# Forgetting heads' values: two of three column chunks, over half of K, as seven block products in place of eight

## The chip, the cores and the metric

The kernel runs on one core of a Trainium2 chip. The metric is the device time of one execution in microseconds, as the median of several runs: 1101.15 us before the change (three runs, 1100.56 to 1102.84). The core has five engines that run their own instruction streams and wait for each other through semaphores: TensorE (PE: matmuls; PEld is its weight load), VectorE (DVE), ScalarE (ACT), GpSimd (POOL) and SyncE (SP). Most transfers are issued by SP, some by POOL; POOL's can add to their destination.

## What is computed

One layer of a hybrid encoder over 256 tokens of width 2048, all in float32: a normed input times one wide matrix, two groups of eight attention heads, an output projection, and a convolutional feed-forward network.

```python
def hybrid_mixer(h, w_in_l, b_forget_l, ...):
    proj = h @ w_in_l          # 256 x 2048 times 2048 x 6152
    qa, ka, va, fa, qb, kb, vb = jnp.split(proj, splits, axis=-1)
    qa = rms_norm(to_heads(qa, N_HEADS_FOX), q_norm_l)
    ka = rms_norm(to_heads(ka, N_HEADS_FOX), k_norm_l)
    log_f = jax.nn.log_sigmoid((fa + b_forget_l).astype(jnp.float32))
    c = jnp.cumsum(log_f, axis=1).transpose(0, 2, 1)
    out_a = forgetting_attention(qa, ka, to_heads(va, N_HEADS_FOX), c)
    ...
```

The change concerns `va`, the values of the eight forgetting heads (1024 columns), which the kernel computes together with the eight columns `fa` of the forget gates: 1032 columns in three chunks of 344.

## The kernel before

**Products in three.** A float32 operand x is kept as a high part hi, rounded to the matmul's format, and a low part lo = x - hi. A product is then three matmuls: token-high by weight-high, token-low by weight-high, token-high by weight-low (`in_three`, L237). Tokens are the stationary operand: `hT[k]`, k = 0 to 15, holds tile k of K (128 rows) with both parts for all 256 tokens; four of them lie in one buffer, hT_76 to hT_79. Weights stream past with up to 512 columns.

**One piece.** `token_major` (L253) goes over K four tiles at a time. For each such piece, `weights` (L230) loads a raw block (`w_raw`, three buffers, issued by SP), and `split` (L213) makes `w_hi` by a cast on ACT (L220) and `w_lo` by a subtraction on DVE (L221), two buffers each. Then come 24 matmuls (L245): 4 tiles x 3 products x 2 halves of the tokens, into the PSUM tile `acc`. A cast can begin only when TensorE has left the high part of two pieces before; a load only when DVE has done the low part of three pieces before.

**The stage.** After an opening that computes the first half's queries, the kernel computes the values (three chunks of four pieces each, L563 on), the first half's keys, the second half's queries and keys (`project`, 512 columns, four pieces each), then the other attention group. Values leave PSUM by `values` (L550): token half 0 as a high and a low part in `vA`, token half 1 in float32 in `vA_rest`. The gates go through `gates` (L576).

**Work beside it.** Small work is written as Python generators that `step()` (L188) moves on by one piece each time; so it is woven between the pieces. `fox_rows` (L332) takes a row set of 512 query or key columns from PSUM (`raw`), squares and sums it over each head on DVE (L343, L345), takes the root (`rsqrt`, L108: two tiny ACT operations, the rest on DVE), rescales (L348), and some steps later transposes it by TensorE (`to_heads`, `ps_h`, L324). `fox_head` (L636) makes scores `ps_s`, weights `pr`, and their transposes `ps_p` (L628), whose high parts ACT and whose low parts DVE (L633) write to `pT`; one step later `weighted` (L606) multiplies them with the values into `ps_o` (L612). Heads go in pairs: 0 and 1, then 2 and 3. `row1` and `R1` (L689, L690) are tiny transfers on POOL that spread `rstd1`, the tokens' norm factors, over all partitions.

**What sets the order.** TensorE runs in the order in which the program is written. On ACT, DVE, SP and POOL a scheduler sets the order when the program is built; `high_priority` moves an instruction ahead in it, `issue_after` holds one behind another. Each engine then runs strictly in that order, and an instruction that waits holds all behind it on its engine.

**Seven in place of eight.** The output projection has such a product already (`in_seven`, L835). A 2 x 2 product of blocks (two halves of the tokens, two halves of K, two halves of the columns) takes eight block products; with sums and differences of token blocks and of weight blocks it takes seven. One block product is 12 matmuls (four tiles of K, three products, one half of the tokens). The token sums are made by DVE and split into `sums` (`block_sums`, `block_parts`); the weight sums are made in place in `w_sum`, in part by POOL's adding transfers.

Of the kernel before, what the change touches and what calls it, by code (L numbers as in the profile page):

```python
# [15 lines left out]
P = 128  # L16
# [30 lines left out]
def hybrid_layer(  # L47
# [59 lines left out]

    def rsqrt(out_, ss, scale, n):  # L108
# [4 lines left out]
        act.activation(y, a, AF.Ln)  # L113
        act.activation(y, y, AF.Exp, scale=-0.5)
        dve.tensor_tensor(u, a, y, op=ALU.mult)
        dve.tensor_tensor(u, u, y, op=ALU.mult)
        dve.tensor_scalar(u, u, -0.5, 1.5, op0=ALU.mult, op1=ALU.add)
        dve.tensor_tensor(out_, y, u, op=ALU.mult)
# [13 lines left out]
    hT = [None] * KT  # L132

    def new_tokens(g):
        t = big.tile([P, 4, 2, S], F32R, name=f"hT{g}", tag=f"hT{g}")
        hT[4 * g : 4 * g + 4] = [t[:, i] for i in range(4)]

# [67 lines left out]
    def load(src):  # L205
        raw = wraw.tile([P, 2048], F32, name="w_raw", tag="w_raw")
        a, b = src.shape[1:]
        nc.sync.dma_start(raw[:, : a * b].rearrange("p (a b) -> p a b", a=a), src)
        return raw

    in_turn, last_split = [], []

    def split(raw, a, b):  # L213
        hi = whi.tile([P, 2048], F32R, name="w_hi", tag="w_hi")
        lo = wlo.tile([P, 2048], F32R, name="w_lo", tag="w_lo")
        n = a * b
        with ExitStack() as turn:
            for ins in in_turn:
                turn.enter_context(tc.issue_after(ins.ins))
            last = [act.copy(hi[:, :n], raw[:, :n])]  # L220
            last.append(dve.tensor_tensor(lo[:, :n], raw[:, :n], f32(hi[:, :n]), op=ALU.subtract))  # L221
        last_split[:] = last
        if in_turn:
            in_turn[:] = last
# [79 lines left out]
    with ExitStack() as actx:  # L304
# [9 lines left out]
        def project(c0, cols):  # L314
            return token_major(lambda k: hT[k], wi, 0, KT, c0, cols)
# [15 lines left out]

        def fox_rows(acc, dst, g, steps=2):  # L332
# [6 lines left out]
            for t in range(NT):  # L339
# [8 lines left out]
                dve.tensor_tensor(r3, r3, r.unsqueeze(2).to_broadcast([P, 4, HD]), op=ALU.mult)  # L348
# [8 lines left out]
        oT_fox = late.tile([P, NH, 2, S], F32R, name="oT_fox")  # L357
        oT = [oT_fox[:, h] for h in range(NH)]
# [4 lines left out]
        def attended(po, h, g, group):  # L363

            if len(done) == NH:
# [175 lines left out]

        qT0 = fox_queries(0)
        waiting.append(fox_rows(acc_q0, qT0, gq, 4))
        step()


        vA_parts = at.tile([P, 2, WF], F32R, name="vA", tag="vA")
        vA = (vA_parts[:, 0], vA_parts[:, 1], vA_rest)
# [8 lines left out]

        lf = at.tile([P, NT, NH], F32, name="lf")
        for j in range(3):
            acc = project(2 * WF + 344 * j, 344)  # L560
            n = 344 if j < 2 else 336
            for t in range(NT):
                if j == 2:  # L563
                    dve.scalar_tensor_tensor(
                        lf[:, t, :], acc[:, t, 336:344], rstd1[:, t : t + 1], bf,
                        op0=ALU.mult, op1=ALU.add,
                    )
            values([v[:, 344 * j : 344 * j + n] for v in vA], acc[:, :, :n])
# [101 lines left out]
        for half in range(2):  # L670
            if half:
                qT = fox_queries(1)
                waiting.append(fox_rows(project(512, 512), qT, gq, 3))
# [4 lines left out]
            waiting.append(fox_rows(project(WF + 512 * half, 512), kT, g_k))  # L678
# [99 lines left out]
        in_order = tc.keep_in_program_order  # L778
        blocks, sums = [], []

        def block_sums():

            for h, tag in enumerate(("minus_c1", "blocks")):
                blocks.append(at.tile([P, 4, S], F32, name=f"oT_blocks{h}", tag=tag))
                some = slice(4 * h, 4 * h + 4)
                in_order(dve.tensor_tensor(
                    blocks[h], f32(oT_fox[:, some, 0, :]), f32(oT_fox[:, some, 1, :]), op=ALU.add
                ))
            a11, a21, a12, a22 = (blocks[h][:, :, t * P : (t + 1) * P] for h in range(2) for t in range(2))
            in_order(dve.tensor_tensor(a11, a11, a21, op=ALU.subtract))  # L790
            in_order(dve.tensor_tensor(a21, a21, a22, op=ALU.subtract))
            in_order(dve.scalar_tensor_tensor(a22, a11, -1.0, a22, op0=ALU.mult, op1=ALU.subtract))
            in_order(dve.tensor_tensor(a12, a12, a22, op=ALU.add))

        def block_parts():
            sums.extend(big.tile([P, NH, S], F32R, name="oT_sums", tag=f"hT{g}") for g in (1, 2))
            places = [[t[:, 4 * h : 4 * h + 4] for t in sums] for h in range(2)]
            for (hi, _), block in zip(places, blocks):
                in_order(act.copy(hi, block))
            for (hi, lo), block in zip(places, blocks):  # L800
                in_order(dve.tensor_tensor(lo, block, f32(hi), op=ALU.subtract))

        for half in range(2):
            qT = sb_queries(half)
            if half:
                block_sums()
# [28 lines left out]
        def in_seven(c0, plus_rg, minus_rg):  # L835

            w11, w12, w21, w22 = (rows_of(wo, 4 * h, 4, c0 + 512 * i, 512) for h in range(2) for i in range(2))
            banks = {}

            def of_heads(h, t):  # L840
                return lambda i, part, _: of_half(oT[4 * h + i], part, t)

            def of_sums(h, t):
                return lambda i, part, _: sums[part][:, 4 * h + i, t * P : (t + 1) * P]

            def plus(into, src):
                with tc.high_priority(offset=AHEAD):
                    nc.gpsimd.dma_start(
                        into.rearrange("p (a b) -> p a b", a=4), src, accum_op=ALU.add
                    )  # L850

            def product(bank, lhs, parts, to, factor=plus_rg):
                new = bank not in banks
                if new:
                    pool, tag = (psb, "t") if bank == "bank_b" else (pss, "s")
                    banks[bank] = pool.tile([P, 512], F32, name=bank, tag=tag)
                in_three([banks[bank]], parts, 4, lhs, new, True, more=not new)
                residual(to[0], c0 + 512 * to[1], banks[bank], factor)

            w, x12 = (  # L860
                pool.tile([P, 2048], F32, name=name, tag=tag)
                for pool, name, tag in ((at, "w_sum", "vA"), (big, "x12", "hT0"))
            )
            with tc.high_priority(offset=AHEAD):
                for into, src in ((w, w11), (x12, w12)):
                    nc.sync.dma_start(into.rearrange("p (a b) -> p a b", a=4), src)
            yield
            yield
            yield
            with tc.issue_after(last_head[0].ins), tc.issue_after(last_head[1].ins):  # L870
                parts = split(w, 4, 512)
                in_order(dve.tensor_tensor(w, w, x12, op=ALU.add))
                block_parts()
            product("bank_a", of_heads(0, 0), parts, (0, 0))
            product("bank_c", of_heads(1, 0), weights(w21, 4, 512), (0, 0))
            yield
            with tc.high_priority(offset=AHEAD):
                parts = split(w, 4, 512)
            plus(w, w22)
            plus(x12, w22)  # L880
            product("bank_b", of_sums(0, 1), parts, (1, 1))
            yield
            product("bank_b", of_sums(1, 0), weights(w22, 4, 512), (0, 1))
            yield
            with tc.high_priority(offset=AHEAD):
                parts = split(w, 4, 512)
            plus(w, w21)
            product("bank_a", of_sums(1, 1), parts, (0, 1), minus_rg)
            yield
            with tc.high_priority(offset=AHEAD):  # L890
                parts = split(x12, 4, 512)
            product("bank_a", of_sums(0, 0), parts, (1, 1), minus_rg)
            yield
            with tc.high_priority(offset=AHEAD):
                parts = split(w, 4, 512)
            product("bank_a", of_heads(1, 1), parts, (1, 0))
# [3 lines left out]
        seven = in_seven(1024, rgs[0], minus_rg)  # L900

        in_turn.extend(last_split)
# [33 lines left out]
    in_turn.clear()  # L936
# [365 lines left out]
```

## Time and profile before

| | |
|---|---|
| median of three runs | 1101.15 us |
| profiled execution, own time | 1100.61 us |
| its span, first to last instruction | 1098.8 us |
| TensorE, DVE, ACT busy | 1094.2, 895.2, 709.3 us |
| granted TensorE clock | 1.0 |
| bytes moved by DMA | 249.04 MB |

The span is 1.8 us shorter than the execution's own time. A row of the timeline gives the start in us from the span's start, the time it took, the engine, the line of the kernel, the operation, what it writes and reads, and the number of equal instructions merged; in brackets stands the idle time of the engine before it and what ended it. A group row gives the busy time, the mean time of one in ns, and the idle time before them. A window row gives the busy time of each engine in that stretch, the granted clock, the mean busy share of the 16 DMA engines, and what they moved. PE rows are modelled to the end of the last matmul, so neighbouring rows overlap by up to 0.2 us.

### The profile page before, as it was taken

What the parts mean: (1) busy time and instruction counts of PE and PEld (TensorE: products, weight loads), DVE (VectorE), ACT (ScalarE), POOL (GpSimd) and SP (SyncE); (2) the same over time, 40 slices, a digit from 0 to 9 for tenths busy, and PEclk for the clock granted to TensorE, in tenths of its full rate; (3) what the DMA queues carried; (4) which work ended last, traced back from release to release, by engine and by line L of the source; (5) the groups of instructions that cost most, each with busy time, mean ns of one, the idle gap of its engine ahead of it and who ended that gap; (6) DMA issues with size and microseconds to landing.
All of it is one profiled execution on the core that took longest, in us unless ns stands there. A gap on an engine that the chain in (4) does not pass through costs nothing.

```text
span 1098.8 us, 14833 instructions
## 1 busy us (share of the span) xinstructions
PE 1094.2 (100%) x5856; PEld 949.3 (86%) x5856; DVE 895.2 (81%) x957; ACT 709.3 (65%) x884; POOL 47.9 (4%) x49
## 2 busy tenths in 40 slices
PE   9999999999999999999999999999999999999998
PEld 7998888888888888888888888888888888888887
DVE  5755777977789776789889988799798889889896
ACT  6544556664665566767757776777676677677753
POOL 0000000000000000001010000100000010100010
PEclk9999999999999999999999999999999999999999
DMA  8776654576639395558999597977979688987985
GB/s 289 183 235 230 190 155 153 192 231 195 226 118 284 110 333 195 168 180 229 278 233 292 191 251 262 259 262 183 320 203 308 211 222 276 248 264 196 324 205 180
DMA packets 180991, 249.04 MB, mean 227 GB/s; under 512 B 4480, under 2 KB 119066, under 8 KB 180666
## 3 DMA queue, kind: packets, MB, share of 16 engines
q1 hardware_dynamic: 162458, 209.67, 58.3%
q0 software_dynamic: 18144, 37.89, 18.4%
q8 instruction: 46, 0.75, 0.3%
q10 hardware_dynamic: 320, 0.53, 0.1%
q14 instruction: 23, 0.19, 0.0%
HBM read 245.97 MB, written 2.11 MB: 226 GB/s over the span
## 4 chain that ended last, share of the span: by engine, by line
PE 100%; ACT 0%; DVE 0%; issue 0%
PE pu L271 34%; PE acc L245 20%; PE pu L277 18%; PE bank_a L245 11%; PE bank_b L245 5%; PE bank_c L245 3%; PE acc L446 2%; PE acc L1180 1%; PE ps_x L146 1%; PE ps_o L612 1%; PE bank_a L1180 1%; PE ps_p L628 0%; PE ps_o L613 0%; PE ps_h L324 0%; PE idle L399 0%; PE ps_s L540 0%
## 5 line engine op out<-in xcount | busy, mean ns | idle before, releaser
L221 DVE TENSOR_TENSOR w_lo<-w_raw,w_hi 128x2048 fp32r<-128x2048 f32 (+1 forms) x194 | 434.9, 2245 | 119.9 <-ACT w_hi L220 119.2
L220 ACT CAST w_hi<-w_raw 128x2048 fp32r<-128x2048 f32 (+1 forms) x194 | 363.6, 1876 | 221.8 <-PE acc L245 61.2
L271 PE MATMUL pu<-hT,w_hi 128*128 128x512 f32 x1664 | 394.0, 390 | 0.0
L271 PEld LDWEIGHTS pu<-hT,w_hi 128*128 128x128 f32 x1664 | 310.3, 188 | 63.1
L277 PEld LDWEIGHTS pu<-hT,w_lo 128*128 128x128 f32 x1664 | 211.9, 191 | 7.0
L277 PE MATMUL pu<-hT,w_lo 128*128 128x256 f32 x1664 | 215.1, 283 | 0.0
L245 PE MATMUL acc<-w_hi,hT 128*128 128x512 f32 (+1 forms) x576 | 124.4, 368 | 0.0
L245 PEld LDWEIGHTS acc<-w_hi,hT 128*128 128x128 f32 x576 | 101.6, 188 | 14.5
L221 DVE TENSOR_TENSOR w_lo<-w_sum,w_hi 128x2048 fp32r<-128x2048 f32 x34 | 77.9, 2290 | 23.1 <-ACT w_hi L220 23.1
L220 ACT CAST w_hi<-w_sum 128x2048 fp32r<-128x2048 f32 x34 | 64.9, 1910 | 46.6 <-PE pu L271 36.4
L997 ACT ACTIVATE tap<-up,ccol 128x256 f32<-128x256 f32 x176 | 74.6, 495 | 0.0
L245 PE MATMUL acc<-w_lo,hT 128*128 128x512 f32 (+1 forms) x288 | 64.6, 366 | 0.0
L245 PEld LDWEIGHTS acc<-w_lo,hT 128*128 128x128 f32 x288 | 51.6, 188 | 7.5
L1102 POOL DMA_DIRECT2D w_sum<-in_w_down_dram x20 | 25.4, 1272 | 678.5 <-DVE w_lo L221 665.4
L245 PE MATMUL bank_a<-w_hi,g 128*128 128x512 f32 x160 | 40.0, 392 | 0.0
L245 PE MATMUL bank_b<-w_hi,s 128*128 128x512 f32 x160 | 40.0, 392 | 0.0
L245 PE MATMUL bank_a<-w_hi,s 128*128 128x512 f32 x160 | 40.0, 392 | 0.0
L245 PEld LDWEIGHTS bank_a<-w_hi,g 128*128 128x128 f32 x160 | 28.9, 189 | 5.3
L245 PEld LDWEIGHTS bank_a<-w_hi,s 128*128 128x128 f32 x160 | 28.9, 189 | 5.3
L245 PEld LDWEIGHTS bank_b<-w_hi,s 128*128 128x128 f32 x160 | 28.9, 189 | 5.3
L1002 DVE TENSOR_TENSOR gate<-gate,tap 128x512 f32<-128x512 f32 x44 | 30.3, 689 | 2.5 <-ACT tap L997 0.2
L1002 DVE TENSOR_TENSOR val<-val,tap 128x512 f32<-128x512 f32 x44 | 30.3, 688 | 2.3
(248 smaller groups left out, 1107.5 us busy)
## 6 DMA issues: line engine op xcount, KB each, us to landing
w_raw<-in_w_up_dram SPq DMA_DIRECT2D x88, 1024.0 KB, 7.6
w_raw<-in_w_down_dram SPq DMA_DIRECT2D x44, 1024.0 KB, 6.0
w_raw<-in_w_in_dram SPq DMA_DIRECT2D x36, 1024.0 KB, 5.5
w_sum<-in_w_down_dram POOLq DMA_DIRECT2D x20, 1024.0 KB, 10.1
w_raw<-in_w_out_dram SPq DMA_DIRECT2D x14, 1024.0 KB, 6.7
w_raw<-in_w_down_dram POOLq DMA_DIRECT2D x10, 1024.0 KB, 14.8
w_raw<-in_w_in_dram SPq DMA_DIRECT2D x12, 688.0 KB, 4.2
w_raw<-in_w_in_dram SPq DMA_DIRECT2D x6, 512.0 KB, 7.0
```

The costliest lines, as they stand in the source:

```text
L146: nc.tensor.transpose(ps[:, j, t * P : (t + 1) * P], xt[t][:, (k + j) * P : (k + j + 1) * P], ident)
L220: last = [act.copy(hi[:, :n], raw[:, :n])]
L221: last.append(dve.tensor_tensor(lo[:, :n], raw[:, :n], f32(hi[:, :n]), op=ALU.subtract))
L245: nc.tensor.matmul(o, lhs(i, l, t), r[:, i, :], start=starts and j == 0, stop=stops and j == 3 * n - 1, skip_group_check=more,)
L271: nc.tensor.matmul(acc[:, j, :], hi[:, i, j * P : (j + 1) * P], hT[k].rearrange("p a b -> p (a b)"), start=k == 0, stop=low_first and k == ...
L277: nc.tensor.matmul(acc[:, j, S:], lo[:, i, j * P : (j + 1) * P], hT[k][:, 0, :], start=False, stop=not low_first and k == KT - 1,)
L446: nc.tensor.matmul(acc[:, t, :], of_half(hT[2 * c + i + j], l, t), r[:, j, :], start=high and c == i == m == 0, stop=not high and c == 7 a ...
L612: nc.tensor.matmul(po, v[j][:, hs], wp[:, k], start=i == 0, stop=False)
L997: act.activation(taps[w][:, j, :], u[:, j, w : w + S], AF.Copy, scale=ccol[:, w, f : f + 1])
L1002: dve.tensor_tensor(a, a, tap, op=ALU.add)
L1102: nc.gpsimd.dma_start(mem[into][:, : nk * 512].rearrange("p (a b) -> p a b", a=nk), src, accum_op=ALU.add)
L1180: nc.tensor.matmul(o, of_half(g, l, t), r[:, i, c0 : c0 + cols], start=kh == 0 and j == 0, stop=kh == n - 1 and j == 11,)
```

## The change

**Values.** Chunks 0 and 1 of the values (columns 0 to 343 and 344 to 687) are computed by `token_major` over tiles 8 to 15 of K only. Over tiles 0 to 7 they are computed by `in_seven`, which is now shared with the output projection and works here on blocks of four tiles of K, 344 columns and 128 tokens. It is a generator (`seven`) that `token_major` moves on by one step after each piece, so its products stand singly between plain pieces of the values, the keys and the second half's queries. Chunk 2, with the gates, stays plain.

```diff
-        for j in range(3):
-            acc = project(2 * WF + 344 * j, 344)
...
+        for c in range(3):
+            k0, nk = (0, KT) if c == 2 else (8, 8)
+            acc = token_major(lambda k: hT[k0 + k], wi, k0, nk, 2 * WF + FIRST * c, FIRST, seven)
             for t in range(NT):
+                if c < 2:
+                    scaled(value_columns[t][c], acc[:, t, :FIRST], t)
+                    continue
```

Called w11, w12, w21, w22 the four weight blocks (first index: half of the eight tiles of K, second: chunk), the sequence is as follows. `in_seven` loads w11 into `w_sum` and w12 into two half buffers `x12` by SP; it multiplies w11 (S1, into bank_a) and w21 (S2, bank_c); DVE adds w12 to `w_sum`; POOL adds w22 to `w_sum` and `x12`, later w21 to `w_sum`; five more products follow, S3 (`w_sum`), S4 (w22), S5 (`w_sum`), S6 (`x12`), S7 (`w_sum`). Each product has its own split, and each is added to the values by a DVE operation.

```diff
+            product("bank_a", of_blocks(0, 0), prepared(lambda: split(w, 4, cols), sum_weights), (0, 0))
+            if not at_once:
+                yield
+                first_loads(moved_x12, (w12,))
+            product("bank_c", of_blocks(1, 0), weights(w21, 4, cols), (0, 0))
...
+            parts = split_ahead(w)
+            moved(nc.gpsimd, w, w22, accum_op=ALU.add)
+            moved_x12(nc.gpsimd, w22, accum_op=ALU.add)
+            product("bank_b", of_sums(0, 1), parts, (1, 1))
+            yield
+            product("bank_b", of_sums(1, 0), weights(w22, 4, cols), (0, 1))
+            yield
+            parts = split_ahead(w)
+            moved(nc.gpsimd, w, w21, accum_op=ALU.add)
+            product("bank_a", of_sums(1, 1), parts, (0, 1), True)
+            yield
+            product("bank_a", of_sums(0, 0), split_ahead(x12), (1, 1), True)
+            yield
+            product("bank_a", of_blocks(1, 1), split_ahead(w), (1, 0))
```

The values are kept in float32 until all products are added; four more casts on ACT and four subtractions on DVE then make the parts in `vA`:

```diff
+            def add(t, h, ps, minus=False):
+                some = value_columns[t][h]
+                factor = (minus_rstd1 if minus else rstd1)[:, t : t + 1]
+                dve.scalar_tensor_tensor(some, ps, factor, some, op0=ALU.mult, op1=ALU.add)
...
+            parts = at.tile([P, 2, WF], F32R, name="vA", tag="vA")
+            for h in range(2):
+                for c0, n, c in ((0, FIRST, FIRST * h), (FIRST, LAST, 2 * FIRST + LAST * h)):
+                    hi, lo = (parts[:, i, c : c + n] for i in range(2))
+                    act.copy(hi, full[h][:, c0 : c0 + n])
+                    dve.tensor_tensor(lo, full[h][:, c0 : c0 + n], f32(hi), op=ALU.subtract)
```

**Squares.** In `fox_rows`, for all four row sets, the squares and their sums move from DVE to ACT:

```diff
-                dve.tensor_tensor(sq, raw, raw, op=ALU.mult)
                 ss = small.tile([P, 4], F32, name="ss", tag="ss")
-                dve.tensor_reduce(ss, sq.rearrange("p (h d) -> p h d", h=4), axis=AX.X, op=ALU.add)
+                for h in range(4):
+                    some = slice(h * HD, (h + 1) * HD)
+                    act.activation(sq[:, some], raw[:, some], AF.Square, accum_out=ss[:, h : h + 1])
```

**Order.** While `ordered[0]` is set, which is now also so from the values to the end of the second half's queries, each split is held behind the last one on ACT and DVE:

```diff
-            for ins in in_turn:
+            for ins in last_split if ordered[0] else ():
                 turn.enter_context(tc.issue_after(ins.ins))
```

The change moves instructions on every engine; the lines shift too (L220 and L221 become L229 and L232, L633 becomes L800, L318 becomes L327). Two places matter below. First, SP's queue at the start of the values. A transfer of 128x4x344 is the raw block of one piece. Before:

```order
L208 DMA w_raw<-in_w_in_dram 128x4x344
L105 DMA masks<-in_cst_dram 128x256
L106 DMA bf<-in_b_forget_dram 128x8
L208 DMA w_raw<-in_w_in_dram 128x4x344 x11
L208 DMA w_raw<-in_w_in_dram 128x4x512 x12
```

And now (`w_sum` receives w11, x_499 and x_500 the halves of w12):

```order
L211 DMA w_raw<-in_w_in_dram 128x4x344
L105 DMA masks<-in_cst_dram 128x256
L106 DMA bf<-in_b_forget_dram 128x8
L211 DMA w_raw<-in_w_in_dram 128x4x344 x2
L612 DMA w_sum<-in_w_in_dram 128x4x344
L211 DMA w_raw<-in_w_in_dram 128x4x344
L612 DMA x_499<-in_w_in_dram 128x2x344
L211 DMA w_raw<-in_w_in_dram 128x4x344
L612 DMA x_500<-in_w_in_dram 128x2x344
L211 DMA w_raw<-in_w_in_dram 128x4x344 x4
L211 DMA w_raw<-in_w_in_dram 128x4x512 x2
L211 DMA w_raw<-in_w_in_dram 128x4x344
```

Three loads without a `w_raw` buffer now stand between those of the pieces, which before were each held until a buffer came free.

Second, ACT and DVE where the second half's keys leave PSUM and heads 2 and 3 get their transposed weights (`pT`). ACT before, and ACT now:

```order
L220 CAST w_hi<-w_raw 128x2048
L318 ACTIVATE raw<-acc,rstd_391 128x512 x2
L631 CAST pT<-ps_p 128x256
L632 COPY pT_1485<-ps_p 128x128
L631 CAST pT<-ps_p 128x256
L632 COPY pT_1494<-ps_p 128x128
L220 CAST w_hi<-w_raw 128x2048
```

```order
L327 ACTIVATE raw<-acc,rstd_390 128x512 x2
L357 ACTIVATE sq,ss<-raw 128x128 x5
L115 ACTIVATE rs_y<-rs_a 128x4
L357 ACTIVATE sq,ss<-raw 128x128
L116 ACTIVATE rs_y<-rs_y 128x4
L357 ACTIVATE sq,ss<-raw 128x128 x2
L798 CAST pT<-ps_p 128x256
L115 ACTIVATE rs_y<-rs_a 128x4
L799 COPY pT_1544<-ps_p 128x128
L116 ACTIVATE rs_y<-rs_y 128x4
L798 CAST pT<-ps_p 128x256
L229 CAST w_hi<-w_raw 128x2048
```

Eight squares and four roots now stand between the row set and the next cast of weights. On DVE the same place before, and now:

```order
L221 TENSOR_TENSOR w_lo<-w_raw,w_hi 128x2048
L343 TENSOR_TENSOR sq<-raw 128x512 x2
L345 TENSOR_REDUCE ss<-sq 128x4 x2
L112 TENSOR_SCALAR rs_a<-ss 128x4
L633 TENSOR_TENSOR pT<-ps_p,pT 128x256
L112 TENSOR_SCALAR rs_a<-ss 128x4
L633 TENSOR_TENSOR pT<-ps_p,pT 128x256
L221 TENSOR_TENSOR w_lo<-w_raw,w_hi 128x2048
```

```order
L361 TENSOR_TENSOR raw<-raw,r 128x512
L117 TENSOR_TENSOR rs_u<-rs_a,rs_y 128x4
L800 TENSOR_TENSOR pT<-ps_p,pT 128x256
L118 TENSOR_TENSOR rs_u<-rs_u,rs_y 128x4
L119 TENSOR_SCALAR rs_u<-rs_u 128x4
L120 TENSOR_TENSOR r<-rs_y,rs_u 128x4
L361 TENSOR_TENSOR raw<-raw,r 128x512
L232 TENSOR_TENSOR w_lo<-w_raw,w_hi 128x2048
L800 TENSOR_TENSOR pT<-ps_p,pT 128x256
```

The low part of head 3's weights (the second `pT`) stood ahead of the low part of the next weight piece, and now stands behind it.

More of the change, by code (lines that the diff above doesn't have):

```diff
@@ L353, in fox_rows @@
             yield
-        oT_fox = late.tile([P, NH, 2, S], F32R, name="oT_fox")
-        oT = [oT_fox[:, h] for h in range(NH)]
+        oT, oT_fox = [], []
         vA_rest = late.tile([P, WF], F32, name="vA_rest", tag="two_heads")
@@ L363, in attended @@
         def attended(po, h, g, group):
+            if not done:
+                oT_fox.append(late.tile([P, NH, 2, S], F32R, name="oT_fox", tag="eight"))
+                oT.extend(oT_fox[0][:, h] for h in range(NH))
             if len(done) == NH:
@@ L672, in hybrid_layer @@
                 qT = fox_queries(1)
[L673 removed]
+                waiting.append(fox_rows(project(512, 512, seven), qT, gq, 3))
+                ordered[0] = False
                 step()
@@ L677, in hybrid_layer @@
             kT = fox_keys(half)
-            waiting.append(fox_rows(project(WF + 512 * half, 512), kT, g_k))
+            waiting.append(fox_rows(project(WF + 512 * half, 512, seven), kT, g_k))
             step()
@@ L776, in sb_head @@
             attended(weighted(v, slice((h % 4) * HD, (h % 4 + 1) * HD), (w, w1)), h, g_sb, 1)
[L778 to L801, printed above, removed]
         for half in range(2):
@@ L805, in hybrid_layer @@
             if half:
-                block_sums()
+                fox_sums = block_sums([oT_fox[0][:, 4 * i : 4 * i + 4] for i in range(2)])
             kT = sb_keys(half)
@@ L833, in residual @@
             dve.scalar_tensor_tensor(xs, ps, factor[:, t : t + 1], xs, op0=ALU.mult, op1=ALU.add)
[L835 to L862, printed above, removed]
-            )
[L864 to L896, printed above, removed]
```

171 lines of the change are left out of this document (147 added, 24 removed).

## The prediction

> **What bounds the kernel now.** I read first the page's busy times and the chain of waits.
>
> ```profile
> PE 1094.2 (100%) x5856; PEld 949.3 (86%) x5856; DVE 895.2 (81%) x957; ACT 709.3 (65%) x884; POOL 47.9 (4%) x49
> PE 100%; ACT 0%; DVE 0%; issue 0%
> ```
>
> TensorE is busy in 1094.2 of 1098.8 us, and the chain that ended last is TensorE throughout. There is no idle time in which a delay could vanish: a matmul taken out is gained, and any wait of TensorE that is put in is paid in full. So I need two things: what the removed products cost, and whether ScalarE (ACT), VectorE (DVE) and the loads still deliver every operand in time. The timeline of TensorE gives the pace (start, us, line, operation, count):
>
> ```profile
> 31.67 2.67 PE L245 MATMUL acc<-w_hi,hT 128*128 128x344 f32 x16
> 34.18 1.43 PE L245 MATMUL acc<-w_lo,hT 128*128 128x344 f32 x8
> 35.44 2.67 PE L245 MATMUL acc<-w_hi,hT 128*128 128x344 f32 x16
> ```
>
> A plain piece of four tiles of K is 24 matmuls of 344 columns, from 31.67 to 35.44: 3.77 us, 0.157 us each.
>
> **Term 1, the products.** Half of K over two chunks is four plain pieces, 96 matmuls; seven block products of 12 are 84. The change removes 12 x 0.157 = 1.9 us, and nothing else leaves TensorE's order. Below I call the plain pieces G0, G1, ... and the block products S1 to S7. With no wait they start at G0 31.67, G1 35.44, G2 39.21, S1 42.98, G3 44.87, S2 48.64, G4 50.53.
>
> **What the other engines get.** The windows of the stage (us, then busy time of PE, PEld, DVE, ACT, POOL, granted clock, DMA share, GB/s):
>
> ```profile
> 31.70:46.80 15.10, 15.10 (x98) 15.08 (x97) 11.39 (x24) 6.66 (x12) 1.84 (x3) 1.00 0.78 141
> 46.80:62.80 16.00, 16.00 (x106) 16.00 (x105) 7.57 (x6) 8.50 (x9) 0.00 (x0) 1.00 0.84 258
> 62.80:78.00 15.20, 15.20 (x98) 15.20 (x98) 7.56 (x5) 6.93 (x7) 0.00 (x0) 1.00 0.74 248
> 78.00:100.40 22.40, 22.40 (x102) 18.13 (x101) 10.78 (x10) 9.91 (x11) 1.59 (x3) 1.00 0.75 247
> L786 DVE TENSOR_TENSOR oT_blocks<-oT_fox 128x1024 f32<-128x1024 f32 x2 | 2.4, 1220 | 0.0
> 51.43 0.57 DVE L554 SCALAR_TENSOR_TENSOR vA<-acc,rstd,vA 128x344 fp32r<-128x344 f32 x1
> 53.29 1.59 DVE L221 TENSOR_TENSOR w_lo<-w_raw,w_hi 128x1376 fp32r<-128x1376 f32 x1 [0.58 <-ACT w_hi L220]
> 48.54 1.35 ACT L220 CAST w_hi<-w_raw 128x1376 fp32r<-128x1376 f32 x1 [5.26 <-DMA w_raw<-in_w_in_dram]
> ```
>
> DVE is busy in 37.3 of 68.7 us, ACT in 32.0. DVE gains three low parts (3 x 1.59), the block sums and their low parts (four operations of 1024 columns at 1.22, four of 512 at about half), two weight sums of 688 (about 0.85 each), seven updates (7 x 0.57) and four small low parts: about 19 us. ACT gains three casts (3 x 1.35), two of 1024, four small ones and the squares of two row sets (below, 6 us): about 14 us. Both still fit, with 12 us and more to spare. So I take all this as hidden, and look for places where the order makes one late operand. I went along each engine's new order, adding these durations, and found three.
>
> **Term 2, the loads of S2 and G4.** Two tiny transfers of `rstd` to DRAM leave POOL at 34.92. Below stand their row of the timeline, three windows around them, then the loads into `w_raw` between 24 and 60 us with their times to landing, and TensorE's row of the piece whose load was latest:
>
> ```profile
> 34.92 1.30 POOL L689 DMA_DIRECT2D row<-rstd  x2 [33.26 <-DVE rstd L118]
> 36.00:37.00 1.00, 1.00 (x8) 1.00 (x7) 1.00 (x1) 0.88 (x2) 0.21 (x1) 1.00 1.05 385
> 38.00:46.00 8.00, 8.00 (x53) 8.00 (x52) 6.98 (x17) 3.24 (x6) 0.54 (x1) 1.00 0.71 29
> 47.00:49.00 2.00, 2.00 (x17) 2.00 (x16) 0.00 (x0) 0.46 (x1) 0.00 (x0) 1.00 1.11 380
> L208 SPq DMA_DIRECT2D w_raw<-in_w_in_dram x9: 367/368/378, 29.1 to 57.1; - x9
> DMA to landing us min/median/max: 4.0/4.4/11.1
> 51.44 2.67 PE L245 MATMUL acc<-w_hi,hT 128*128 128x344 f32 x16
> ```
>
> From 2.6 us after their issue, for some 9 us, the queues move 29 GB/s in place of 380. Before the change one load falls into this: it lands after 11.1 us, its cast waits 5.26 us for it (48.54 above), and its matmuls start at 51.44, 1.5 us after that cast's end. The old kernel stood just clear of this hole. The new one asks for more bytes ahead of it: SP now sends G2 (from 29.1), w11, G3, half of w12, w21 (S2), the other half of w12, G4. A chunk of 688 KB is 0.70 MB, 1.85 us at 380 GB/s. With the first landing at 33.1 (29.1 + 4.0) come w11 at 34.9 and G3 at 36.8. The hole opens about 1 us earlier, near 36.4, because `rstd` now stands ahead of the second low part on DVE; until 45.4 it lets through 0.27 MB. What is left of G3 and w12's half ends near 46.0, w21 at 47.9, w12's rest at 48.8, G4 at 50.6. Each cast adds 1.35: S2's high part is ready at 49.25, 0.6 after 48.64; G4's at 51.95, 0.8 after its start thus shifted. I take 1.4 us. If the hole shuts a microsecond sooner it is 0.4, without the hole 0 (ACT and DVE alone are in time there); a microsecond later, 2.6.
>
> **Term 3, the keys' transposes.** Their rows were finished 0.8 us before use (109.17 + 1.29 against 111.28):
>
> ```profile
> 109.17 1.29 DVE L348 TENSOR_TENSOR raw<-raw,r 128x512 f32<-128x512 f32 x2
> 111.28 1.03 PE L324 MATMUL ps_h<-cs,raw 128*128 128x128 f32 x8
> ```
>
> Two block products now lie between (3.8 us more room), but ACT has squares, a further cast and the value casts there, and DVE's second rescaling stands behind a low part of 2.2 us. Adding up, it ends 0.3 us late; bounds 0 and 0.8.
>
> **Term 4, head 3's weights.** This is the largest, and lies outside the seven products: `fox_rows` now squares on ACT, eight pieces of 128 with their sums in place of two DVE pairs. Where the last of the row sets, the second half's keys, falls beside heads 2 and 3, the engines stood so (rows of the timeline of ACT, DVE, TensorE; then two exponentials on ACT):
>
> ```profile
> 150.24 1.26 ACT L318 ACTIVATE raw<-acc,rstd 128x512 f32<-128x512 f32 x2
> 151.38 0.37 ACT L631 CAST pT<-ps_p 128x256 fp32r<-128x256 f32 x1
> 152.06 0.30 ACT L632 COPY pT<-ps_p 128x128 f32<-128x128 f32 x1
> 154.51 1.91 ACT L220 CAST w_hi<-w_raw 128x2048 fp32r<-128x2048 f32 x1 [2.16 <-PE pu L271]
> 156.33 0.29 ACT L113 ACTIVATE rs_y<-rs_a 128x4 f32<-128x4 f32 x2
> 155.44 0.42 DVE L633 TENSOR_TENSOR pT<-ps_p,pT 128x256 fp32r<-128x256 f32 x1
> 156.49 2.29 DVE L221 TENSOR_TENSOR w_lo<-w_raw,w_hi 128x2048 fp32r<-128x2048 f32 x1 [0.63 <-ACT w_hi L220]
> 158.69 0.23 DVE L115 TENSOR_TENSOR rs_u<-rs_a,rs_y 128x4 f32<-128x4 f32 x2
> 156.73 0.61 PE L612 MATMUL ps_o<-pT,vA 128*128 128x256 f32 x3
> 125.00 0.39 ACT L658 ACTIVATE pr<-pr,nm 128x128 f32<-128x128 f32 x1
> 125.39 0.50 ACT L659 ACTIVATE pr<-pr,nm 128x256 f32<-128x256 f32 x1
> ```
>
> Before, both heads' low parts (`pT`, L633 on DVE) were done at 155.86, the weight's low part followed, and head 3's matmuls began at 156.73. In the new order DVE has the second `pT` behind `w_lo` of 2048, and `w_lo` needs ACT's cast. That cast could not start before 154.51 (TensorE frees its buffer), and now stands behind the squares. In the old clock: rows end at 151.38; eight squares of 128 with a sum, at the 0.39 from one exponential's start to the next (125.00 to 125.39), are 3.1; four tiny roots some 0.45 (0.11 apart); the `pT` copies 0.7: the cast starts at 155.65 and ends at 157.55; `w_lo` takes 2.2 (156.49 to 158.69) to 159.8, `pT` 0.4 to 160.2. Head 3's second matmul, the first to read it, was due at 156.85. TensorE, in order, waits 3.4 us, with all behind it. If the squares were fast enough to clear the cast, order alone leaves 159.1, 2.3 us. If a square takes 0.5, it is 4.2. I take 3.3, nearer the 0.39 row. A shift of everything before this place shifts both sides alike, so earlier stalls give no cover.
>
> **The accumulating transfers** I cost at nothing. POOL adds w22, then w21, into `w_sum`:
>
> ```profile
> L848 POOL DMA_DIRECT2D w_sum<-in_w_out_dram x2: 1268/1270/1271, 335.2 to 351.9; - x2
> DMA to landing us min/median/max: 8.7/10.4/12.1
> ```
>
> There 1024 KB land in 8.7 to 12.1 us; here they are 688 KB. From one use of `w_sum` to the next lie two block products and two plain pieces of 512 columns (5.44 each, 24 x 0.227): 14.7 us of TensorE, plus the 2 us by which the low part leads. Cover 3 us or more. If it were gone, each microsecond late costs one.
>
> **The sum:** -1.9 + 1.4 + 0.3 + 3.3 = +3.1 us; by the bounds from +0.4 (-1.9 + 0 + 0 + 2.3) to +5.7 (-1.9 + 2.6 + 0.8 + 4.2). The profiled execution took 1100.61 us (1.8 outside the span), the median of the runs is 1101.15. So 1103.7 against the first, 1104.2 against the median.
>
> **The rivals.**
>
> - *The hole is covered* (+1.7 us, 1102.9): terms 1, 3 and 4 alone. For it: the exact length of the hole decides, and I have one sample. Against: 2.1 MB are sent before G3 has landed, where 1.4 were. 0.16.
> - *Full saving, not slower* (-1.9 us, 1099.3): DVE reaches the second `pT` before the weights' low part counts, and the loads keep their lead. Its place is 156.73; it decides from the point where `w_lo` starts 3.4 us sooner than I reckon. Against it: the cast was released by TensorE only at 154.51 even before. 0.04; with only one of the two waits gone for good (no wait at the heads, 1100.9) another 0.03.
> - *TensorE loses its pace after the long wait* (1105.9). In the opening, after idling, 14 matmuls of 256 columns took 3.17 us:
>
> ```profile
> 1.06 3.17 PE L399 MATMUL idle<-zeros 128*128 128x256 bf16 x14 [1.06 <-DVE zeros L389]
> 154.32 2.08 PE L277 MATMUL pu<-hT,w_lo 128*128 128x256 f32 x16
> ```
>
>   That is 0.21 each against 0.12 later, for about 4 us: 1.7 us lost. If a wait of 3.4 us sets TensorE back to it, it costs 1.7 more. Against: no wait in this trace is long enough to show it. 0.06. The Trainium skill, "TensorE: Matmul & The Clock Gate", Part 1, has the rule: the clock is halved after an idle window of 3413 ns, free-running; by it a gap of about that length seldom fills a whole window, and the trace here shows only the opening's slow pace.
> - *The accumulations come late* (1108): landing twice as slow, 21 us against 17, twice. 0.05.
>
> **The numbers.** Forecast 0.66, with its own range 1102.4 to 1106.2. Predicted 1104.2. Reaching down to the covered hole and half-way to the lower cases, up past the slow pace: 1101.4 to 1107.0. About 0.2% (2.2 us) is what a measurement can tell; slower begins at 1103.35. Slower: 0.53 of the forecast, 0.04 of the covered hole, the two last rivals 0.11: 0.68. Faster, below 1098.95: half of the full saving, 0.02, and a little of scatter: 0.04. Same: 0.28.
>
> **What would show it.** TensorE idle at head 3's `ps_o` matmul, released by DVE's `pT`, 2.3 to 4.2 us: term 4. Idle before bank_c and the next plain piece, released by ACT's cast that itself waited for a load: term 2; released by DVE instead, my load ledger is wrong. A small gap at `ps_h`: term 3. 5844 matmuls in place of 5856. A gap before bank_a would be the late accumulations. Wrong altogether if TensorE stays without gaps.

## The result, and the profile after

| | before | after |
|---|---|---|
| median | 1101.09 us (9 runs, 1100.56 to 1102.84) | 1104.93 us (9 runs, 1102.57 to 1106.36) |
| profiled execution, own time and span | 1100.61, 1098.8 us | 1106.03, 1104.3 us |
| matmuls | 5856 | 5844 |

The ratio is 1.0032, with a 95% interval of 1.0022 to 1.0043: slower by 3.8 us. The page's line of busy times, and the line of the cores with the span and the mean granted clock of TensorE:

```profile
PE 1095.9 (99%) x5844; PEld 949.7 (86%) x5844; DVE 904.1 (82%) x964; ACT 725.4 (66%) x959; POOL 53.0 (5%) x53
core 0: 1104.3 us, clock 0.998
```

TensorE lost its 12 matmuls and yet is busy 1.7 us longer, in a span that is 5.5 us longer. So two things happened: it waited, and it ran for a while at another pace; the clock of 0.998, 1.0 before, says the second. The page's chain of waits breaks off after some 7% of the span here and carries nothing. I go by the timeline of TensorE instead, at the four places of the prediction. First the start of the values (start, us, line, operation; in brackets the idle time and what ended it), then what ACT waited for there:

```profile
48.11 1.43 PE L254 MATMUL acc<-w_lo,hT 128*128 128x344 f32 x8
49.38 1.43 PE L254 MATMUL bank_c<-w_hi,hT 128*128 128x344 f32 x8
50.65 0.80 PE L254 MATMUL bank_c<-w_lo,hT 128*128 128x344 f32 x4
51.91 2.78 PE L254 MATMUL acc<-w_hi,hT 128*128 128x344 f32 x16 [0.46 <-ACT w_hi L229]
46.05 1.35 ACT L229 CAST w_hi<-w_raw 128x1376 fp32r<-128x1376 f32 x1 [2.08 <-DMA w_raw<-in_w_in_dram]
50.52 1.34 ACT L229 CAST w_hi<-w_raw 128x1376 fp32r<-128x1376 f32 x1 [3.11 <-DMA w_raw<-in_w_in_dram]
```

S2 (bank_c, 49.38) is not late: its cast waited 2.08 us for the load and still ended 2 us ahead. G4 (51.91) is: its cast waited 3.11 us for its load. The rows overlap by their modelled ends, so the loss is read from starts: four low-part matmuls take 0.63 (half of the 1.27 from 48.11 to 49.38), G4 was due at 51.28 and is 0.63 late.

Then the keys' transposes, with DVE's rescaling of the rows:

```profile
110.97 0.60 PE L333 MATMUL ps_h<-cs,raw 128*128 128x128 f32 x4
111.94 0.66 PE L333 MATMUL ps_h<-cs,raw 128*128 128x128 f32 x4 [0.37 <-DVE raw L361]
108.48 2.29 DVE L232 TENSOR_TENSOR w_lo<-w_raw,w_hi 128x2048 fp32r<-128x2048 f32 x1
111.19 0.69 DVE L361 TENSOR_TENSOR raw<-raw,r 128x512 f32<-128x512 f32 x1
```

Four transposes take 0.41 in the second row set (111.94 to 112.35, the next piece's start), so the second four were due at 111.38: 0.56 late, behind a rescaling that itself stood behind the low part of 108.48.

These two small waits are not steady. In two more profiled executions of the same kernel (they stand below, under the clock's grid) G4 began 0.38 us late (at 50.99) and on time (at 51.49), and the eight transposes ran through as before (110.07 to 110.86, 110.46 to 111.25).

Then head 3, on TensorE, ACT and DVE:

```profile
156.47 0.52 PE L779 MATMUL ps_o<-pT,vA 128*128 128x256 f32 x3
156.97 0.36 PE L779 MATMUL ps_o<-pT,vA 128*128 128x256 f32 x1
159.87 0.50 PE L779 MATMUL ps_o<-pT,vA 128*128 128x256 f32 x2 [2.54 <-DVE pT L800]
160.35 3.54 PE L286 MATMUL pu<-hT,w_lo 128*128 128x256 f32 x16
163.69 2.60 PE L280 MATMUL pu<-hT,w_hi 128*128 128x512 f32 x10
151.62 0.31 ACT L357 ACTIVATE sq<-raw 128x128 f32<-128x128 f32 x1
151.92 0.30 ACT L357 ACTIVATE sq<-raw 128x128 f32<-128x128 f32 x1
155.00 0.36 ACT L798 CAST pT<-ps_p 128x256 fp32r<-128x256 f32 x1
155.25 1.91 ACT L229 CAST w_hi<-w_raw 128x2048 fp32r<-128x2048 f32 x1
157.19 2.29 DVE L232 TENSOR_TENSOR w_lo<-w_raw,w_hi 128x2048 fp32r<-128x2048 f32 x1 [0.34 <-ACT w_hi L229]
159.40 0.42 DVE L800 TENSOR_TENSOR pT<-ps_p,pT 128x256 fp32r<-128x256 f32 x1
```

This is the queue that term 4 described: squares on ACT, then the weight's cast at 155.25, DVE's `w_lo` at 157.19 only after it, and head 3's `pT` behind `w_lo`. TensorE's second matmul of head 3 was due at 157.12 and began at 159.87: 2.7 us. Behind it the 16 matmuls of `pu` take 3.34 us (160.35 to 163.69) in place of the 2.0 that such a row takes elsewhere. The windows there (us; busy PE, PEld, DVE, ACT, POOL; granted clock; DMA share; GB/s) show why:

```profile
157.00:160.00 3.00, 0.46 (x4) 0.26 (x4) 2.81 (x3) 0.72 (x3) 0.00 (x0) 1.00 0.21 74
160.00:161.00 1.00, 1.00 (x8) 1.00 (x9) 0.55 (x2) 0.75 (x2) 0.00 (x0) 0.81 0.37 38
161.00:162.00 1.00, 1.00 (x7) 1.00 (x7) 0.57 (x2) 0.45 (x2) 0.00 (x0) 0.50 0.86 201
163.00:164.00 1.00, 1.00 (x6) 1.00 (x5) 0.00 (x0) 0.00 (x0) 0.00 (x0) 0.50 1.04 369
164.00:165.00 1.00, 1.00 (x6) 0.77 (x5) 0.00 (x0) 0.00 (x0) 0.00 (x0) 0.99 0.30 95
```

From 160.62 to 164.03 the clock is halved: 3.41 us, in which about 1.5 us of work is lost (the offset of TensorE's starts against the kernel before grows by that much, from 3.0 to 4.5). This is the third rival, the loss of pace, on top of the forecast. Of the 5.4 us between the two profiled executions, 0.6, 0.6, 2.7 and 1.5 lie at these places; the rest beyond what the products save is the opening, 0.7 us longer in this run, and about 1 us of small differences behind 1087 us, among them a gap of 0.25 before the last column block; its cause stays open.

### The profile page after: what moved, and what is told of

It is laid out like the page before. It is cut to its first block, busy times and chain, and to the rows that moved or that the text cites. A ratio compares the mean times of both kernels' runs of the same rounds, so it can differ in the third digit from the quotient of the medians.

```text
span 1104.3 us, 14902 instructions
## 1 busy us (share of the span) xinstructions
PE 1095.9 (99%) x5844; PEld 949.7 (86%) x5844; DVE 904.1 (82%) x964; ACT 725.4 (66%) x959; POOL 53.0 (5%) x53
## 5 line engine op out<-in xcount | busy, mean ns | idle before, releaser
L232 DVE TENSOR_TENSOR w_lo<-w_raw,w_hi 128x2048 fp32r<-128x2048 f32 (+1 forms) x192 | 431.9, 2253 | 106.6 <-ACT w_hi L229 104.3
L229 ACT CAST w_hi<-w_raw 128x2048 fp32r<-128x2048 f32 (+1 forms) x192 | 360.9, 1882 | 209.6 <-PE pu L280 57.3
L254 PE MATMUL acc<-w_hi,hT 128*128 128x512 f32 (+1 forms) x512 | 113.7, 374 | 0.5 <-ACT w_hi L229 0.5
L254 PEld LDWEIGHTS acc<-w_hi,hT 128*128 128x128 f32 x512 | 91.4, 188 | 15.0 <-ACT w_hi L229 0.7
L232 DVE TENSOR_TENSOR w_lo<-w_sum,w_hi 128x2048 fp32r<-128x2048 f32 (+1 forms) x38 | 84.2, 2216 | 22.2 <-ACT w_hi L229 22.0
L229 ACT CAST w_hi<-w_sum 128x2048 fp32r<-128x2048 f32 (+1 forms) x38 | 70.3, 1850 | 46.4 <-PE pu L280 36.9
L254 PE MATMUL acc<-w_lo,hT 128*128 128x512 f32 (+1 forms) x256 | 58.9, 372 | 0.0
L254 PEld LDWEIGHTS acc<-w_lo,hT 128*128 128x128 f32 x256 | 46.4, 188 | 7.5
```

Source lines behind the costliest of these rows:

```text
L229: copied = act.copy(hi[:, some], r[:, :m])
L232: rest = dve.tensor_tensor(lo[:, some], r[:, :m], f32(hi[:, some]), op=ALU.subtract)
L254: nc.tensor.matmul(o, lhs(i, l, t), r[:, i, :], start=starts and j == 0, stop=stops and j == 3 * n - 1, skip_group_check=more,)
```

## The experiments

Medians stand beside runs of the kernel before on the same chip: 1101.05 us for the first four, 1100.89 for the next two, 1100.86 for the last four.

**Squares back on DVE, block products kept.**

```diff
+                dve.tensor_tensor(sq, raw, raw, op=ALU.mult)
...
-                for h in range(4):
-                    some = slice(h * HD, (h + 1) * HD)
-                    act.activation(sq[:, some], raw[:, some], AF.Square, accum_out=ss[:, h : h + 1])
+                dve.tensor_reduce(ss, sq.rearrange("p (h d) -> p h d", h=4), axis=AX.X, op=ALU.add)
```

> The changed kernel with the squares of fox_rows back on DVE; the seven products stay. Theory A (the loss is head 3's wait, which the squares on ACT make by way of the order, and the slow clock that follows it; the seven products gain): no wait at ps_o, granted clock 1.0, the small waits at bank_c/acc (0.5 us) and ps_h stay; -1.9 + 0.6 + 0.4 = about 1100.2 us against 1101.1 before. Rival B (the seven products cost by their splits, updates and adding transfers, the squares are harmless): 1104 to 1105, as the changed kernel.

1100.21 us (1099.35 to 1102.18), ratio 0.9995 [0.9986, 1.0004], clock 1.0 in all 11 runs. TensorE and DVE at the heads:

```profile
155.41 0.60 PE L778 MATMUL ps_o<-pT,vA 128*128 128x256 f32 x3
155.99 2.16 PE L286 MATMUL pu<-hT,w_lo 128*128 128x256 f32 x16
157.99 3.82 PE L280 MATMUL pu<-hT,w_hi 128*128 128x512 f32 x16
154.12 0.42 DVE L799 TENSOR_TENSOR pT<-ps_p,pT 128x256 fp32r<-128x256 f32 x1
155.17 2.29 DVE L232 TENSOR_TENSOR w_lo<-w_raw,w_hi 128x2048 fp32r<-128x2048 f32 x1 [0.64 <-ACT w_hi L229]
```

The second `pT` (154.12) is again ahead of `w_lo`, and nothing waits. So the block products by themselves are not what made the kernel slower; with the squares where they were, the change cannot be told from no change. I had expected the two small waits to stay, and both were gone: G4 began on time (at 50.85), although the tiny transfers were still there and the queues moved 121 GB/s from 38 to 46 us, and the transposes lost 0.1 us. So the median at the expected 1100.2 is in part luck: the products saved less than I had put in, and the waits that were to eat it did not come. This run also gives the price of the products, from start to start of each on TensorE:

```profile
43.26 1.43 PE L254 MATMUL bank_a<-w_hi,hT 128*128 128x344 f32 x8
45.16 2.68 PE L254 MATMUL acc<-w_hi,hT 128*128 128x344 f32 x16
72.46 1.50 PE L254 MATMUL bank_b<-w_hi,hT_sums 128*128 128x344 f32 x8
74.44 3.83 PE L254 MATMUL acc<-w_hi,hT 128*128 128x512 f32 x16
```

Five of the seven take 1.89 to 1.90 us (43.26 to 45.16), the two in bank_b 1.98 and 1.99 (72.46 to 74.44): 13.45 in all, against 15.08 for four plain pieces. The saving is 1.6, not 1.9; the offset against the kernel before falls by 1.5 from the stage's start to 125 us.

**Only the squares on ACT, plain pieces kept** (the kernel before, with the opposite edit).

> The kernel before with only the squares of fox_rows moved to ACT; no seven products for the values. Theory A: TensorE waits 2.5 to 3 us at head 3's ps_o for DVE's pT, and the clock is halved for some 3.4 us after it: 1101.1 + 2.7 + 1.6 = about 1105.4. Rival B: 1101 to 1101.5, no wait there.

1104.9 us (1103.67 to 1105.43), ratio 1.0034 [1.0022, 1.0046]: a loss as large as the changed kernel's, without any block product. By what the products save, less its two small waits, the changed kernel should be up to 1.6 us ahead of this one; the runs of the two, 11 and 22 in all, scatter by 2.7 and 3.8 us, and it is not to be seen. The wait is the same one:

```profile
156.75 0.36 PE L613 MATMUL ps_o<-pT,vA 128*128 128x256 f32 x1
159.65 0.50 PE L613 MATMUL ps_o<-pT,vA 128*128 128x256 f32 x2 [2.54 <-DVE pT L634]
160.13 2.16 PE L277 MATMUL pu<-hT,w_lo 128*128 128x256 f32 x16
```

In this profile the 16 matmuls behind it took 2.0 us (160.13 to 162.13): the clock did not fall here. It did in three of the five runs (0.998).

**Block products and squares on ACT, but the heads' weights ahead.** Only the place of three operations in the order of ACT and DVE is given anew; others beside them shift with it, and TensorE's order stays:

```diff
-            act.copy(w[:, 0], pt0)
-            copied = act.copy(w1, pt[:, 2, :])
-            last_head[:] = [copied, dve.tensor_tensor(w[:, 1], pt0, f32(w[:, 0]), op=ALU.subtract)]
+            with tc.high_priority(offset=2 * AHEAD):
+                act.copy(w[:, 0], pt0)
+                copied = act.copy(w1, pt[:, 2, :])
+                last_head[:] = [copied, dve.tensor_tensor(w[:, 1], pt0, f32(w[:, 0]), op=ALU.subtract)]
```

> The changed kernel, squares still on ACT, but the heads' transposed weights (pT) with a higher priority, so that both stand ahead of the next weight piece's low part on DVE. Theory A: the wait at ps_o goes or falls below 0.5 us, clock 1.0, about 1100.3 us. If the squares' load on ACT and not the order were what counts (rival C): the wait only moves to the next cast of weights, 2 us or more there, and the time stays near 1104.

1100.55 us (1099.05 to 1101.04), ratio 0.9994 [0.9985, 1.0003], clock 1.0 (once 0.999).

```profile
151.91 0.75 DVE L801 TENSOR_TENSOR pT<-ps_p,pT 128x256 fp32r<-128x256 f32 x2
156.10 2.29 DVE L232 TENSOR_TENSOR w_lo<-w_raw,w_hi 128x2048 fp32r<-128x2048 f32 x1 [0.90 <-ACT w_hi L229]
156.03 0.60 PE L779 MATMUL ps_o<-pT,vA 128*128 128x256 f32 x3
156.61 2.16 PE L286 MATMUL pu<-hT,w_lo 128*128 128x256 f32 x16
```

All of ACT's squares are still there, and the wait at head 3 is gone (the one at G4 stayed, 0.36 us idle): it is the order behind the squares, not their time, that costs there. Both `pT` are done over 3 us ahead, as they stand before the squares now.

**Zeros into the wait.** 20 matmuls of 256 columns on zeros into head 3's `ps_o`, ahead of its own products (the first of these overwrites them):

```diff
+            for _ in range(fill):
+                nc.tensor.matmul(po, zeros[:, :P], zeros, start=True, stop=True)
```

> The changed kernel with 20 dummy matmuls of 256 columns (bf16 zeros, about 2.2 us) written into head 3's ps_o just ahead of its products: the wait is filled, not removed. If the halved clock is set off by TensorE's idleness (theory A): the place still costs 2.7 us but the clock stays at 1.0 in all runs, 1.6 us faster than the changed kernel, about 1103.2, and the runs scatter less. If the slow clock has another cause (rival D): 1104.9 as the changed kernel, clock 0.998.

1103.73 us, ratio 1.0023 [1.0013, 1.0032]; one execution of 4155.52 us was disturbed and is left out of the ratio. The clock was 0.998 in one of ten runs, where I had expected none; that run (1107.46 us) has no profile, and why it was so slow stays open.

```profile
155.46 2.35 PE L779 MATMUL ps_o<-zeros 128*128 128x256 bf16 x20
158.32 0.50 PE L781 MATMUL ps_o<-pT,vA 128*128 128x256 f32 x2 [0.39 <-DVE pT L802]
158.79 2.15 PE L286 MATMUL pu<-hT,w_lo 128*128 128x256 f32 x16
```

`pT` comes no sooner, but TensorE is idle for 0.39 us only, and the clock stays in nine of the ten runs, while the unfilled kernel has 0.998 or less in 15 of 22 (below). So the fall goes with the idle time.

**No tiny transfers.** `R1` is made by TensorE, two matmuls of 128 columns and a copy on DVE:

```diff
-        rstd1, _ = token_factors(ss1, 1, diagonal=False)
+        rstd1, dg1 = token_factors(ss1, 1)
...
-            row1 = dram.tile([NT, P], F32, name="row1")
-            for t in range(NT):
-                nc.gpsimd.dma_start(row1[t : t + 1, :].rearrange("t p -> p t"), rstd1[:, t : t + 1])
-            nc.gpsimd.dma_start(R1, row1.rearrange("t p -> (t p)").unsqueeze(0).to_broadcast([P, S]))
+            R1 = in_every_partition(dg1, 1, at)
```

> The changed kernel with R1 made by TensorE (two matmuls of 128 columns and one copy on DVE) in place of the tiny transfers of rstd to DRAM and back; the squares stay on ACT. Building it anew also moves DVE's low part of 2048 columns at heads 2 and 3 to behind the second pT. Theory (the tiny transfers make the hole that delays G4's load; the wait at head 3 comes from the order on DVE, not from the squares by themselves): the queues move over 300 GB/s between 38 and 46 us, no wait of TensorE at G4, none at head 3's ps_o, granted clock 1.0 throughout; 1104.9 less 0.5 less 2.6 less 1.6, plus 0.3 for the two matmuls: 1100.5 us, 1100.0 to 1101.0. Rival (the load is late because of the bytes ahead of it): the rate stays, at 130 GB/s, and G4 still waits about 0.4 us. Rival (the squares' time on ACT itself delays head 3): a gap of over 1 us stays at ps_o and the time is over 1102.5.

1100.37 us (1099.97 to 1101.08), ratio 0.9997 [0.9988, 1.0006], as expected. Windows of this kernel, then of the changed one:

```profile
38.00:40.00 2.00, 2.00 (x14) 2.00 (x13) 1.24 (x7) 2.00 (x8) 0.00 (x0) 1.00 1.06 374
40.00:42.00 2.00, 2.00 (x15) 2.00 (x14) 1.92 (x4) 1.25 (x5) 0.00 (x0) 1.00 1.06 377
44.00:46.00 2.00, 2.00 (x14) 2.00 (x13) 2.00 (x3) 1.21 (x1) 0.00 (x0) 1.00 0.00 0
```

```profile
38.00:40.00 2.00, 2.00 (x15) 2.00 (x14) 1.24 (x8) 2.00 (x11) 0.00 (x0) 1.00 1.85 258
40.00:42.00 2.00, 2.00 (x15) 2.00 (x14) 1.96 (x2) 1.62 (x5) 0.00 (x0) 1.00 0.76 87
44.00:46.00 2.00, 2.00 (x15) 2.00 (x14) 2.00 (x2) 0.00 (x0) 0.55 (x1) 1.00 0.43 105
```

Without the tiny transfers the queues run at 374 to 377 GB/s until the loads are through, and then stand empty (0 from 44 us). My expected mean of over 300 GB/s up to 46 us was wrong for that reason: 202, since there was nothing left to move. G4's cast (47.94) waited for TensorE and for no load, and TensorE had no gap there. The wait at head 3 is gone too: ACT has the squares, but the order on DVE now puts `pT` (ended at 155.06) ahead of `w_lo` (155.99). A gap of 0.25 us at the keys' transposes stayed (0.44 late, reckoned as above). As two things changed here, the hole and DVE's order, the time alone says nothing of the hole: with the order put right and the tiny transfers kept it was 1100.55.

**The same with the squares back on DVE.**

> As the run before, with the squares and their sums back on DVE. Theory: with hole, squares and order all as they should be, nothing of TensorE waits but about 0.1 us at the keys' transposes; the saving of the products stands alone: 1101.05 less 1.9 plus 0.3 for the two added matmuls plus 0.4 for what single products lose by switching banks: 1099.9 us, 1099.4 to 1100.4, so not to be told from the kernel with the squares on DVE and the tiny transfers (1100.2), which had no early gap. Rival (the transfers cost TensorE time that no gap shows): over 0.5 us better than that kernel, below 1099.6.

1100.2 us (1099.84 to 1101.51), ratio 0.9995 [0.9986, 1.0004]; no gap at any of the four places (the transposes took 0.1 us longer than before). It is the same time as with the tiny transfers (1100.21): once nothing waits, removing the hole brings nothing. None of these versions is shown to beat the kernel before, as all their intervals reach over 1.

**The clock's grid.** The changed kernel twice more, the kernel with only the squares moved once more, and the changed kernel with 10 matmuls on zeros in place of 20:

> The changed kernel once more, unchanged, for the records of its clock. Theory (the clock is judged once in every 3.41 us, on a grid that is fixed by the moment of the opening's rise to full clock, and falls when TensorE was idle for most of one such stretch): with the wait of 2.5 us at head 3, work out from the rise the stretches of 3.413 us and the part of each that is idle; with 74% or more idle the clock is 0.5 for the next 3.41 us and the time 1.6 us longer, with 46% or less it stays 1.0. Rival (whether it falls has nothing to do with that grid): falls and idle parts do not agree.

> The same kernel and the same two theories: a second sample of the grid's place. By chance about 7 in 10 such runs should show the fall.

> The kernel before with only the squares moved to ACT, once more, for its clock's record. The same two theories: its wait of 2.5 us lies 0.2 us earlier, its grid elsewhere; 74% idle or more in one stretch and the clock falls, 46% or less and it does not.

> The changed kernel with 10 matmuls on zeros ahead of head 3's products in place of the 20 of the fill before: they take about 1.05 us, so about 1.45 us of the wait stay idle, at most 43% of any stretch of 3.41 us. Theory: the clock never falls, granted clock 0.999 or 1.0 in all runs, 1103.3 us, 1102.5 to 1104.0, as with 20. Rival (any wait of over a microsecond lets the clock fall): granted clock 0.998 in most runs and 1104.9 us.

The trace records when the clock rises in the opening and when it falls. From the rise I count on in steps of 3.413 us, and take TensorE's idle part of the step that has most of it (us from the span's start):

| profiled run | rise | idle | fullest step | idle part | clock falls at |
|---|---|---|---|---|---|
| changed | 7.02 | 157.33 to 159.87 | 157.20 to 160.62 | 74% | 160.62 |
| changed, second | 5.55 | 155.81 to 158.38 | 155.74 to 159.15 | 75% | 159.15 |
| changed, third | 6.33 | 156.20 to 158.78 | 156.51 to 159.93 | 66% | 159.93 |
| squares alone, second | 4.17 | 157.38 to 159.92 | 157.77 to 161.19 | 63% | 161.19 |
| squares alone, first | 5.08 | 157.11 to 159.65 | 155.27 to 158.68 | 46% | no fall |
| half the fill | 6.37 | 158.10 to 159.58 | 156.56 to 159.97 | 43% | no fall |

The times of the first three were 1104.91, 1103.45 and 1104.42 us (ratios 1.0034 [1.0020, 1.0047], 1.0022 [1.0012, 1.0033], 1.0031 [1.0019, 1.0044]). In all four falls of the table the fall lies on the grid, at the end of the step that was mostly idle, and lasts one step; in the other two no step was half idle and nothing fell. My expectation left open what happens between 46% and 74% idle; 66% and 63% gave a fall. Half the fill left 1.48 us of waiting, and none of its ten runs shows a clock under 0.999 (1103.81 us, ratio 1.0021 [1.0012, 1.0031]). Over the 22 runs of the changed kernel, 15 have a clock of 0.998 or less with a median of 1104.91 us, and 7 have 0.999 or 1.0 with a median of 1103.11. The two medians lie 1.8 us apart; in the four profiled executions that have the fall, TensorE's starts lose 1.5 to 1.6 us by it. Which execution has it depends on where the grid lies, and the rise moved by up to 2.85 us between the six.

## Why the prediction was right, step by step

The forecast, 1104.2 us and slower, came out within 0.7 us of the median. The mechanism was right at the largest term. That the number came so close is partly luck: the four terms, +3.1 as forecast, came to +1.2 to +2.3, and a loss of pace that the forecast had left out made up for it.

- **Term 1, the products:** -1.9 forecast, -1.6 measured. The removed matmuls are worth what they cost before, but the two products in bank_b cost 0.1 more each than half a piece. That they follow a tiny product for the gates is in the trace; that this is the cause was not tried.
- **Term 2, the loads:** +1.4 forecast; +0.6 measured in the first profiled execution, 0.4 and 0 in the two others, at G4 alone. The hole is there, and that the tiny transfers make it is shown by the kernel without them. That the hole by itself makes G4 wait is not shown: G4 was on time in one of these three executions and in the kernel with the squares on DVE, with the hole in both. My ledger let only 0.27 MB through the hole, as before the change, where 25 to 34 GB/s went through; with the new order it was 81 to 105 between 40 and 46 us, so S2's load came 2 us earlier than I reckoned. G4's cast began at 50.52, and I had its load land at 50.6; but the opening took 0.7 us longer in this execution (G0 began at 32.35), and the loads left later by nearly as much (29.69 against 29.05), so it too was some 0.7 us early. The step that failed is the rate in the hole, which I took over from the kernel before.
- **Term 3, the transposes:** +0.3 forecast; +0.56 measured in the first profiled execution, inside its bounds, released by DVE's second rescaling as said; nothing in the two others.
- **Term 4, head 3's weights:** +3.3 forecast, 2.7 to 2.8 measured in all three profiled executions, at the place, behind the instructions and with the releaser that were named. The size that was off is the square: I took 0.39 us from exponentials of the same width, and the trace shows 0.30 (151.62 to 151.92), which for eight of them is the 0.7. The three kernels without this wait (1100.21, 1100.55, 1100.37) and the one with it alone (1104.9) bear the term out.
- **The accumulating transfers:** nothing, as forecast, but by less than the 3 us of cover that I counted: the cast of S7 waited 1.11 us for `w_sum`, and TensorE for nothing.
- **The loss of pace:** I gave it 0.06 as a rival, and it was there in 15 of 22 runs. The four terms as measured come to +2.3 in the first profiled execution (-1.6 + 0.6 + 0.6 + 2.7) and to +1.6 and +1.2 in the two others; the runs whose clock stayed have a median of 1103.11, 2.0 above the kernel before. The fall adds 1.5 to 1.8 in most runs, and the median is theirs. My price of 1.7 was near (by the row that I showed it should have been 1.9, as 14 matmuls in 3.17 us are 0.23 each and not 0.21), and the chance was wrong. The step that failed is "a gap of about that length seldom fills a whole window": it need not fill one. 63% idle sufficed and 46% did not; 2.54 us can cover 74% of 3.41, so most places of the grid give a fall. The Trainium skill, "TensorE: Matmul & The Clock Gate", Part 1, is right here about the length of the window and its free run; that the window has to be idle throughout, as I read it, the runs contradict.

So the 1.6 us that the change saves on TensorE were more than spent, mostly by an edit that has nothing to do with the seven products: the squares moved to ACT, which delayed one cast, which with the order on DVE delayed head 3's weights, and in that wait the clock fell.

## What to carry to other kernels

Where TensorE has no slack, work that moves to an engine with spare time is priced by what stands behind it in that engine's order and who waits for that: eight squares of 0.3 us cost nearly 4 us here, and nothing that the runs could tell once three operations stood ahead of them. And a wait of TensorE can cost more than its length: with 2.5 us of waiting the clock was low in 15 of 22 runs, at 1.5 to 1.8 us each, and with 1.5 us in none of ten. Ask how much of one step of 3.41 us a wait may take up; here 63% was enough and 46% was not.

## What was not expected of the hardware

- The clock of TensorE falls to half for one step of 3.413 us after a step that was 63% idle or more, in steps counted from the opening's rise; 46% left it alone. Where between the two the limit lies stays open.
- Two transfers of 0.5 KB each, 128 elements of 4 bytes, landed about 9 us after their issue and held the other queue to 25 to 34 GB/s for 8 us in the kernel before; in the changed one they landed after about 10 us, with 81 to 105 GB/s between 40 and 46 us, where more loads were in flight. That the number of loads in flight makes the difference was not tried.
